# Attention beside eight products instead of eleven: four steps a pair, placed by half products, and two gated products ahead of it and two behind

## The chip, the cores and the metric

The kernel runs on one core of one Trainium2 chip. The metric is the device time of one launch in microseconds (us). A core has TensorE (PE in the profile, with PEld for its weight loads), VectorE (DVE), ScalarE (ACT), GpSimd (POOL) and SyncE (SP, which only issues transfers), and 16 DMA engines that move data between DRAM and the on-chip memory. TensorE writes its sums to eight banks of PSUM.

## What is computed

One layer over 1024 tokens of 1024 channels, all float32. The reference, cut:

```python
h = rmsnorm(x, norm_g)
q, k, v, za, u, vs, zs, gm = split(h @ w_in)
q, k = partial_rope(q), partial_rope(k)           # 16 query heads, 2 key heads, 64 wide
a   = window_sink_attention(q, k, v, sinks)        # 64-token chunks; a chunk sees itself and two before
a   = (a * silu(za)) @ w_att_out
sgo = chunked_spatial_gating(gelu(u), gelu(vs), sg_w, sg_b, ln_g, ln_b)
sgo = (sgo * silu(zs)) @ w_sg_out
ga, gs = split(sigmoid(gm + b_merge))
y = ga * a + gs * sgo
x = x + y @ w_o
return rmsnorm(x, final_g)
```

## The kernel before

**Products.** Every big product is made in pairs of 128 output rows. A pair takes seven half-size products (a seven-product scheme for a 2 by 2 block), named after the right-hand form that each uses: b11, t1, t2, b21, t3, b22, t4. A float32 operand is split into a high and a low part of the reduced type fp32r (lines L155 on ACT and L156 on DVE, results `wh` and `wl`), and `product` (L343, its matmul at L351) adds high x high, high x low and low x high over four blocks of 128: 12 matmuls of 128x512. Two of the weights' parts are used as they are (`r0`, `r1`, loaded to `wr`), two more are sums of parts (`sa`, `sb`, tile `s`), made by DVE (`pair_job`, L251 to L255) or beforehand in DRAM by accumulating transfers on POOL's queue (`early_job`, L300; the steps at L306 are handed out one by one by `part_of_early` and wait for the latest PSUM copy of ACT).

**Order of the stages.** vs; u (gated mixing, gives `s1_dr`); k and v; q; one pair of zs, silu at once and times `s1_dr`; then eleven pairs with attention beside them: the other three pairs of zs (stored raw in `zr_dr`), four of gs, four of ga; then four pairs of za with silu and times the attention (`at_dr`); then the products with w_sg_out, w_att_out and w_o. In the za stage `gate_raw` (L1462) also brings back `zr_dr` and `s1_dr`, takes silu on ACT (L1468), multiplies on POOL (L1472) and stores `s_dr`.

**Attention.** It has 32 steps (2 key heads x 8 blocks of 128 tokens x 2 halves of the heads). A step n is a chain over three engines:

- `scores` (PE L1109, 8 matmuls into two banks `ps_sc`)
- `maxima` (DVE L1134 to L1137, once for each of two chunks c)
- `exponentials` (ACT L1145 to L1153)
- `weigh` (DVE L1158 to L1165: sum, reciprocal and the weights of chunk 0; ACT L1167: chunk 1)
- `turn` (PE L1180, L1185: transposes into the two banks `ps_tp`)
- `casts` (ACT L1196, L1202) and `inner_rest`, `ends_rest` (DVE L1208, L1216): the split into high and low part
- `values` (PE L1233, into one bank `ps_o`)
- `outputs` (ACT copy L1246, DVE add L1247, and every second step a store to `at_dr` on POOL's queue)

`locked_pair` (L1260) writes a pair's seven products and three steps b, c and most of a in a fixed order: PE, ACT and DVE run this part in written order, while the other stages are ordered by a scheduler. Between two products stands whatever PE owes the attention; in front of t2 and b21 for instance:

```python
of(values, a)
mm(acc, 3, "t2", False)
of(weigh, b)
of(outputs, a)
x22 = xtile()
pace[0] = nc.scalar.mul(x22[:], t5, -1.0)
if p:
    split_next()
    ...
of(turn, b)
t2 = bank("o")[:]
mm(t2, 1, "b21", True)
x12 = xtile()
pace[0] = nc.scalar.copy(x12[:], acc)
of(casts, b)
```

The query tile of step n is loaded two steps ahead on SP's queue (two buffers `q`).

Of the kernel before, what the change touches and what calls it, by code (L numbers as in the profile page):

```python
# [31 lines left out]
P = 128  # L32
# [21 lines left out]
def hybrid_tile(  # L54
# [67 lines left out]
    zr_dr = scratch("zr_dr")  # L122
# [71 lines left out]
    sums_to_make = []  # L194
    locked = [False]
# [90 lines left out]

    early = []
# [12 lines left out]
    def early_job(n, i0, i1):  # L300
# [18 lines left out]
        def job():  # L319
            r0, r1 = raw_tile(), raw_tile()  # L320
            sa = mtile([P, D], F32, "s", 2)
            sb = mtile([P, D], F32, "s", 2)
            copy_to(r0[:], w[i0])
            for a, dst in enumerate((sa, sb)):
                copy_to(
                    dst[:].rearrange("p (b n) -> p b n", b=2),
                    made[:].rearrange("p (b a) n -> p a b n", a=2)[:, a],
                )
            copy_to(r1[:, HALF:D], w[i1][:, HALF:D])
            return [  # L330
                (r0[:], [(n, 0), (n, 1)]),
                (sa[:], [(n, 2), (n, 3)]),
                (sb[:], [(n, 4), (n, 5)]),
                (r1[:, HALF:D], [(n, 6)]),
            ]
# [24 lines left out]
    def gemm_pair(b, finish, hook=lambda: None, second="o"):  # L360
# [5 lines left out]
        acc = bank("mm")[:]  # L366
        x11, x12, x22 = xtile(), xtile(), xtile()
        product(acc, ready[n, 0], b["b11"], True)
# [51 lines left out]
    ahead_of = {}  # L420
    for base, step, made in (
        (W_U, 1, 0),
        (W_Q, 0, 0),
        (W_ZS, 1, 0),
        (W_SG, 2, KC),
        (W_ATT, 2, KC),
        (W_ZA, 1, 0),
        (W_SG + 1, 2, KC // 2),
        (W_ATT + 1, 2, KC // 2),
    ):  # L430
        if base == W_Q:
            jobs.append(pair_job(len(jobs), of_kv))
        for m in range(0, KC, 2):
            i0, i1 = base + step * m, base + step * (m + 1)
            if m < made:
                ahead_of[len(jobs)] = True
                jobs.append(early_job(len(jobs), i0, i1))
            else:
                load = of_w(i0, i1) if step else of_token_w(base, m)
                jobs.append(pair_job(len(jobs), load))  # L440
    N_PAIRS = len(jobs)
# [427 lines left out]
    def rope_tables():  # L869

        cos_sb = mtile([P, NT, 16], F32, "cos", 1, pool)
        sin_sb = mtile([P, NT, 16], F32, "sin", 1, pool)
        nc.sync.dma_start(cos_sb[:], cos)
        nc.sync.dma_start(sin_sb[:], sin)
        yield
        for src in (cos_sb[:, :, 0:8], sin_sb[:, :, 8:16]):
            tab = mtile([P, HALF], F32, f"tab{len(tables)}", 1, pool)
            wide = []
            for i in range(4):
                v = mtile([P, 2, 8, 8], F32, "wide", 4, pool)  # L880
                nc.vector.tensor_copy(v[:], src[:, i : i + 5 : 4, :].unsqueeze(2).broadcast_to([P, 2, 8, 8]))
                wide.append(v)
            yield
            pt = bank("tp")
            for i, v in enumerate(wide):
                nc.tensor.transpose(pt[:, i * P : (i + 1) * P], v[:].rearrange("p a h d -> p (a h d)"), ident[:])
# [162 lines left out]
    def first_loads():  # L1049
        for n in range(2):  # L1050
# [4 lines left out]
    gates, silus, hooked = [], [], [0]  # L1055

    def gate_of_zs(i, half, q, src, sign):
        nc.scalar.activation(q[:], src, AF.Silu, scale=sign)
        silus.append((i, half, q))

    def part_of_zs():
        part_of_q()
        hooked[0] += 1
        if hooked[0] == 1:
            two = mtile([P, 2, HALF], F32, "qhl", 3, pool)
            copy_to(two[:].rearrange("p h n -> p (h n)"), s1_dr[0:P, :])
            gates.extend((two[:, 0, :], get(s1_dr, 1, 1, 5, "rot")[:], two[:, 1, :]))
        if hooked[0] == 5:
            gates.append(get(s1_dr, 1, 0, 5, "rot")[:])
        if hooked[0] >= 4:  # L1070
            while silus:
                i, half, q = silus.pop(0)
                nc.vector.tensor_mul(q[:], q[:], gates.pop(0))
                put(s_dr, i, half, q[:])

    steps_of_q += [rotate(1, 1), first_loads()]
    gemm_pair(hb, gate_of_zs, part_of_zs)
# [18 lines left out]
    def scores(n):  # L1096
# [19 lines left out]
        if n + 2 < len(steps):  # L1116
            qT.append(query_stage(*steps[n + 2]))
# [21 lines left out]
    def exponentials(n):  # L1139

        st = held[n]
        for c in range(2):
            lo, hi = window_of(st.t, c)
            for i in range(2):
                nc.scalar.activation(  # L1145
                    st.pr[:, i, place_of(c, lo, hi)],
                    st.sc[c][:, i, lo:hi],
                    AF.Exp,
                    bias=st.nmax[:, c, i : i + 1],
                    scale=-1.0,  # L1150
                    accum_out=st.sums[:, c, i : i + 1],
                )
        nc.scalar.activation(st.es[:], st.es[:], AF.Exp)  # L1153
# [106 lines left out]
    def locked_pair(p, finish):  # L1260


        a, b, c, d = range(3 * p - 1, 3 * p + 3)
# [5 lines left out]
        def mm(acc, at, form, fresh):  # L1269
            product(acc, ready[n, at], hb[form], fresh)  # L1270
            part_of_early(1 if p < 3 else 2)
# [558 lines left out]
```

## Time and profile before

| | |
|---|---|
| median of three runs | 942.9 us (941.05 to 943.75) |
| the profiled execution's own time | 940.39 us |
| its span | 938.4 us, so 2.0 us lie around it |
| PE busy | 909.4 us, 97% |
| DVE / ACT / POOL busy | 691.8 / 529.7 / 150.3 us |
| granted TensorE clock, mean | 0.992 |
| moved by DMA | 212.9 MB |

Busy time of PE is modelled: a matmul of 128x512 is shown about 0.39 us long but the next one starts some 0.23 us later, so a gap on PE shows up about 0.16 us short. In a row of the timeline the first two figures are start and length, and in brackets stands the idle time of the engine just before with what ended it.

### The profile page before, as it was taken

How to read it: one execution, taken by the hardware profiler on the slowest of the kernel's cores; microseconds unless marked ns; L12 is line 12 of the kernel's file. 1: busy time of each engine (PE TensorE's matmuls, PEld its weight loads, DVE VectorE, ACT ScalarE, POOL GpSimd, SP SyncE). 2: the span in 40 equal slices, each digit the busy share in tenths (PEclk: the TensorE clock that was granted, in tenths of full speed). 3: DMA queues.
4: the chain of work that ended last, by engine and by line, in shares of the span. 5: the costliest groups of instructions: out<-in, count | busy, mean ns of one | idle time of the engine just before them, and what ended most of it. 6: DMA issues, size and time to landing. Idle time of an engine off the chain costs nothing.

```text
span 938.4 us, 13120 instructions
## 1 busy us (share of the span) xinstructions
PE 909.4 (97%) x4285; PEld 751.4 (80%) x4285; DVE 691.8 (74%) x1222; ACT 529.7 (56%) x1050; POOL 150.3 (16%) x199
## 2 busy tenths in 40 slices
PE   7999999999999899999999999998999999999996
PEld 5788888888888778888888888876787887878885
DVE  5784776665677677777777777765799689668996
ACT  6873333334445457777667767754385565457443
POOL 1002222213011022211001111024010011210012
PEclk9999999999999999999999999999999999999998
DMA  6237678877688799998888999279888664999623
GB/s 248 100 112 218 197 145 186 184 152 225 232 291 265 220 268 250 254 246 227 260 265 270 226 254 273 73 285 372 305 278 310 213 200 151 261 298 334 203 106 120
DMA packets 130620, 212.91 MB, mean 227 GB/s; under 512 B 12696, under 2 KB 59288, under 8 KB 130552
## 3 DMA queue, kind: packets, MB, share of 16 engines
q1 hardware_dynamic: 110312, 157.28, 50.8%
q0 software_dynamic: 20096, 54.54, 25.3%
q8 instruction: 34, 0.56, 0.3%
q14 instruction: 34, 0.28, 0.1%
q10 hardware_dynamic: 144, 0.26, 0.1%
HBM read 152.13 MB, written 93.45 MB: 262 GB/s over the span
## 4 chain that ended last, share of the span: by engine, by line
PE 46%; DMA 8%; DVE 6%; issue 3%; ACT 2%; SPq 0%; POOL 0%; ACTq 0%; DVEq 0%; POOLq 0%
PE ps_mm L351 20%; PE ps_o L351 15%; PE ps_sc L1109 3%; PE ps_sc L351 2%; PE ps_o L1233 2%; PE ps_tp L351 2%; DMA q<-q_hl 2%; DMA g<-at_dr 1%; PE ps_tp L1180 1%; DVE wl L156 1%; DMA wr<-in_w_dram 1%; DMA s_dr<-bq 1%; DMA bq<-zr_dr 1%; DVE bq L185 1%; DMA v<-v_dr 1%
## 5 line engine op out<-in xcount | busy, mean ns | idle before, releaser
L156 DVE TENSOR_TENSOR wl<-wr,wh 128x1024 fp32r<-128x1024 f32 (+1 forms) x80 | 77.9, 975 | 50.6 <-ACT wh L155 49.8
L155 ACT CAST wh<-s 128x1024 fp32r<-128x1024 f32 (+1 forms) x67 | 66.4, 996 | 83.5 <-PE ps_mm L351 32.4
L155 ACT CAST wh<-wr 128x1024 fp32r<-128x1024 f32 (+1 forms) x80 | 65.5, 829 | 65.6 <-PE ps_mm L351 33.6
L156 DVE TENSOR_TENSOR wl<-s,wh 128x1024 fp32r<-128x1024 f32 (+1 forms) x67 | 77.9, 1164 | 19.2 <-ACT wh L155 19.1
L1145 ACT ACTIVATE pr<-ps_sc,sm 128x192 f32<-128x192 f32 (+2 forms) x128 | 51.3, 408 | 56.2 <-DVE sm L1135 55.4
L351 PE MATMUL ps_mm<-T_b11h,wl 128*128 128x512 f32 x140 | 55.6, 397 | 5.5 <-DVE wl L156 5.5
L306 POOL DMA_DIRECT2D sums<-in_w_dram x48 | 36.3, 957 | 148.4 <-PE ps_mm L587 64.0
L351 PE MATMUL ps_o<-T_t1h,wh 128*128 128x512 f32 x148 | 58.9, 398 | 1.0 <-ACT wh L155 0.9
L351 PE MATMUL ps_o<-T_b22h,wh 128*128 128x512 f32 x148 | 58.4, 395 | 0.0
L351 PE MATMUL ps_o<-T_t1h,wl 128*128 128x512 f32 x148 | 58.1, 393 | 0.2
L351 PE MATMUL ps_o<-T_t1l,wh 128*128 128x512 f32 x148 | 57.9, 391 | 0.0
L351 PE MATMUL ps_o<-T_b22h,wl 128*128 128x512 f32 x148 | 57.8, 391 | 0.0
L351 PE MATMUL ps_o<-T_b22l,wh 128*128 128x512 f32 x148 | 57.8, 391 | 0.0
L351 PE MATMUL ps_mm<-T_b11h,wh 128*128 128x512 f32 x140 | 55.3, 395 | 1.6 <-ACT wh L155 1.6
L351 PE MATMUL ps_mm<-T_t4h,wh 128*128 128x512 f32 x140 | 56.2, 401 | 0.7 <-DVE x L386 0.7
L351 PE MATMUL ps_mm<-T_t4h,wl 128*128 128x512 f32 x140 | 55.3, 395 | 0.0
L351 PE MATMUL ps_mm<-T_t4l,wh 128*128 128x512 f32 x140 | 55.3, 395 | 0.0
L351 PE MATMUL ps_mm<-T_t3h,wh 128*128 128x512 f32 x140 | 55.2, 394 | 0.0
L351 PE MATMUL ps_mm<-T_b11l,wh 128*128 128x512 f32 x140 | 55.1, 394 | 0.0
L351 PE MATMUL ps_mm<-T_t3h,wl 128*128 128x512 f32 x140 | 54.8, 391 | 0.0
L351 PE MATMUL ps_mm<-T_t2h,wl 128*128 128x512 f32 x140 | 54.7, 390 | 0.0
L351 PE MATMUL ps_mm<-T_t2l,wh 128*128 128x512 f32 x140 | 54.6, 390 | 0.0
(365 smaller groups left out, 2474.0 us busy)
## 6 DMA issues: line engine op xcount, KB each, us to landing
wr<-in_w_dram SPq DMA_DIRECT2D x80, 256.0 KB
sums<-in_w_dram POOLq DMA_DIRECT2D x24, 512.0 KB, 5.6
s<-sums SPq DMA_DIRECT2D x24, 512.0 KB
wr<-in_w_dram SPq DMA_DIRECT2D x16, 512.0 KB
q_hl<-qhl SPq DMA_DIRECT2D x16, 512.0 KB
q<-q_hl SPq DMA_DIRECT2D x64, 128.0 KB
y_dr<-x POOLq DMA_DIRECT2D x28, 256.0 KB, 6.1
sums<-in_w_dram POOLq DMA_DIRECT2D x24, 256.0 KB, 9.8
```

What stands on the lines that cost most here:

```text
L155: nc.scalar.copy(hi, src)
L156: return nc.vector.tensor_sub(lo, src, hi.bitcast(F32))
L185: op(dst[:, i : i + 2, :], a[:, i : i + 2, :], c[:, i : i + 2, :])
L306: return lambda: paced(nc.gpsimd.dma_start(dst, src, accum_op=op))
L351: nc.tensor.matmul(acc, lt, rt, start=fresh and k == 0 and n == 0, stop=k == 3 and n == 2, skip_group_check=True,)
L1109: nc.tensor.matmul(sc[:, i, lo:hi], q_of[:, c, i * P : (i + 1) * P], kt[:, f, lo:hi], start=f == 0, stop=f == 1,)
L1145: nc.scalar.activation(st.pr[:, i, place_of(c, lo, hi)], st.sc[c][:, i, lo:hi], AF.Exp, bias=st.nmax[:, c, i : i + 1], scale=-1.0, accum_o ...
L1180: nc.tensor.transpose(st.inner[0:wide, at : at + P], st.pr[:, i, place_of(c, 64 if st.t else P, 192)], ident[:])
L1233: nc.tensor.matmul(st.po[:, cs], lt, rt, start=i == 0, stop=i == len(terms) - 1, skip_group_check=True)
```

## The change

Attention now runs beside the eight pairs of gs and ga alone, four steps a pair. Two pairs of zs stand in front of it and two behind, all with silu at once and the product with `s1_dr` on DVE; `zr_dr`, `gate_raw` and POOL's multiplies are gone. Inside a pair the work of attention is hung at six places: ahead of products and, by the new argument `middle` of `product`, after half of one. `t2` takes an `mm` bank, so that the one free `ps_o` bank serves the attention. The exponentials of a step are issued a chunk at a time. Query tiles are loaded three steps ahead (three buffers). The sums of the third zs pair are made in DRAM as well (13 early jobs instead of 12), seven early steps go beside the second zs pair, and the loads of sums are issued after t2. The tables of the rotation share buffers with `rot`. At the end the first product of the third zs pair stands between the last steps of attention.

The diff, cut to its core:

```diff
-    def product(acc, part, form, fresh, last=True):
+    def product(acc, part, form, fresh, middle=lambda: None):
         for k in range(4):
+            if k == 2:
+                middle()
...
+    add_pairs(W_ZS, 1, (0, 2))
+    add_pairs(W_SG, 2, ALL, True)
+    add_pairs(W_ATT, 2, ALL, True)
+    add_pairs(W_ZS, 1, (4,), True)
+    add_pairs(W_ZS, 1, (6,))
+    add_pairs(W_ZA, 1, ALL)
...
-        qt = mtile([P, 4, P], F32R, "q", 2, aheads)
+        qt = mtile([P, 4, P], F32R, "q", 3, aheads)
...
-    steps_of_q += [rotate(1, 1), first_loads()]
-    gemm_pair(hb, gate_of_zs, part_of_zs)
+    steps_of_q += [first_loads(), rotate(1, 1)]
+    zs_pair(0, part_of_q)
+    zs_pair(2, with_early)
+    after(nc.scalar.activation(warm[:], eps_sb[:], AF.Exp), last_silu[0])
...
-        a, b, c, d = range(3 * p - 1, 3 * p + 3)
+        y, z, a, b, c, d = range(4 * p - 2, 4 * p + 4)
...
-            part_of_early(1 if p < 3 else 2)
+            part_of_early(1 if p < 5 else 2)
...
+        of(scores, a)
+        of(turn, z)
+        of(values, y)
+        def h0():
+            of(outputs, y)
+            of(casts, z)
+            of(inner_rest, z)
+            of(maxima, a, 0)
+            of(ends_rest, z)
+            of(maxima, a, 1)
+            of(exponentials, a, 0)
+            of(exponentials, a, 1)
+        multiply(acc, 0, "b11", True, h0)
+        for tail in tails:
+            tail()
...
+        def h2():
+            of(weigh, a)
+            of(values, z)
+            of(outputs, z)
+            x11 = held["x11"] = xtile()
+            pace[0] = nc.scalar.copy(x11[:], acc)
+            of(scores, b)
+        multiply(t5, 2, "t1", True, h2)
+        of(maxima, b, 0)
+        of(maxima, b, 1)
+        of(exponentials, b, 0)
         of(turn, a)
+        def h4():
+            of(casts, a)
+            of(inner_rest, a)
+            of(exponentials, b, 1)
+            of(ends_rest, a)
+        multiply(acc, 3, "t2", False, h4)
         of(weigh, b)
         if p:
             split_next()
+        load_made()
+        t2 = bank("mm")[:]
+        def h6():
+            x12 = held["x12"] = xtile()
+            pace[0] = nc.scalar.copy(x12[:], acc)
+            of(values, a)
+            of(outputs, a)
+            hold.append(split_next(True))
+            of(turn, b)
+            of(scores, c)
+        multiply(t2, 1, "b21", True, h6)
...
+        multiply(acc, 4, "t3", False, h8)
         of(values, b)
         of(weigh, c)
...
         of(scores, d)
+        def h10():
+            of(maxima, d, 0)
+            of(maxima, d, 1)
+            of(exponentials, d, 0)
+            of(turn, c)
+            hold.pop()()
+        multiply(t5, 5, "b22", False, h10)
+        of(exponentials, d, 1)
+        of(casts, c)
+        of(weigh, d)
...
-        for dst in (zr_dr, gs_dr, ga_dr):
-            for m in range(2 if dst is zr_dr else 0, KC, 2):
+        for dst in (gs_dr, ga_dr):
+            for m in range(0, KC, 2):
                 locked_pair(p, rest(dst, m))
...
-            nc.gpsimd.tensor_tensor(z[:, 0:2, :], z[:, 0:2, :], z[:, 2:4, :], op=ALU.mult)
-            copy_to(s_dr[j * P : (j + 1) * P, :], z[:, 0:2, :].rearrange("p h n -> p (h n)"))
...
+    want_gates(s1_dr, 4)
+    silu_pair(4, s_dr, (s1_dr, 6))
+    silu_pair(6, s_dr, (at_dr, 0))
     for m in range(0, KC, 2):
...
+        silu_pair(m, a_dr, (at_dr, m + 2) if m < 6 else None)
```

What this does to the order of the engines is shown at three places. The first is ACT, early in a pair of the middle of attention. Before, from the tail of the pair in front (`x` from `ps_mm`, L490) over the copy of an output (L1246), a copy of a sum (L1295), the casts of one step and the exponentials of the next to that step's weighing (L1167):

```order
L490 ACTIVATE x_4954<-ps_mm_4627 128x512
L1246 COPY aT_4836<-ps_o_4929 64x2x4x64
L1295 COPY x_5004<-ps_mm_4934 128x512
L1196 CAST pT_5006<-ps_tp_4965 128x512
L1202 CAST pTb_5008<-ps_tp_4970 64x256 x2
L1145 ACTIVATE pr_4990,sm_4987<-ps_sc_4973,sm_4986 128x192 x2
L1145 ACTIVATE pr_4990,sm_4987<-ps_sc_4978,sm_4986 128x192 x2
L1153 ACTIVATE sm_4988<-sm_4988 128x4
L1167 ACTIVATE pr_4990<-pr_4990,sm_4989 128x192 x2
```

And now the same stretch for steps z, a and b of the second pair (L1275 is the copy of an output, L1334 of a sum, L1173 exponentials, L1225 and L1231 casts, L1196 the weighing, L154 the cast of a split):

```order
L1275 COPY aT_3293<-ps_o_3348 64x2x4x64
L1334 COPY x_3361<-ps_mm_3266 128x512
L1173 ACTIVATE pr_3382,sm_3379<-ps_sc_3363,sm_3378 128x192 x2
L1225 CAST pT_3411<-ps_tp_3397 128x512
L1231 CAST pTb_3413<-ps_tp_3402 64x256 x2
L1173 ACTIVATE pr_3382,sm_3379<-ps_sc_3368,sm_3378 128x192 x2
L1182 ACTIVATE sm_3380<-sm_3380 128x4
L1196 ACTIVATE pr_3382<-pr_3382,sm_3381 128x192 x2
L154 CAST wh_3435<-s_2915 128x1024
```

The first chunk's exponentials have moved ahead of the casts of the step before. The second place is PE around the product b21 of the same kind of pair. Before, the transposes of step b (L1180, L1185) stand alone ahead of the product:

```order
L351 MATMUL ps_mm_4627<-T_t2l_781,wh_4603 128x512
L351 MATMUL ps_mm_4627<-T_t2h_780,wl_4604 128x512
L1180 MATMUL ps_tp_4754<-ident,pr_4678 128x128 x4
L1185 MATMUL ps_tp_4759<-ident,pr_4678 128x128 x2
L351 MATMUL ps_o_4762<-T_b21h_143,wh_4520 128x512
```

Now, in the middle of the product, stand the values of a (L1262), the transposes of b (L1209, L1214) and the scores of c (L1138):

```order
L364 MATMUL ps_mm_3443<-T_b21h_143,wl_3175 128x512
L1262 MATMUL ps_o_3453<-pT_3411,vi_3171 128x512 x2
L1262 MATMUL ps_o_3453<-pTb_3413,v_3168 128x256 x2
L1209 MATMUL ps_tp_3463<-ident,pr_3382 128x128 x4
L1214 MATMUL ps_tp_3468<-ident,pr_3382 128x128 x2
L1138 MATMUL ps_sc_3471<-k_3187,q_3189 128x192 x4
L1138 MATMUL ps_sc_3476<-k_3187,q_3189 128x192 x4
L364 MATMUL ps_mm_3443<-T_b21h_143,wh_3174 128x512
```

Three groups that stood apart are now one, half a product later. The third place is ACT in the first pair after attention. Before, silu of the raw zs (`bq`, L1468) stands among silu of za (`x`, L1490) and the casts of splits (`wh`):

```order
L376 COPY x_6187<-ps_mm_6185 128x512
L1468 ACT_TABLE_LOAD
L1468 ACTIVATE bq_6176<-bq_6176 128x1024
L1490 ACTIVATE x_6186<-x_6186 128x512
L155 CAST wh_6268<-wr_6157 128x1024
L1468 ACTIVATE bq_6179<-bq_6179 128x1024
L1490 ACTIVATE x_6188<-x_6188 128x512
L155 CAST wh_6314<-s_6239 128x1024
```

Now the same place holds the third pair of zs, with silu on its own sums (L1527):

```order
L392 COPY x_5945<-ps_mm_5886 128x512
L154 CAST wh_6004<-wr_5519 128x1024
L1527 ACT_TABLE_LOAD
L1527 ACTIVATE x_5944<-x_5944 128x512
L1527 ACTIVATE x_5946<-x_5946 128x512
L154 CAST wh_6050<-s_5979 128x1024
L1527 ACTIVATE x_5945<-x_5945 128x512
L154 CAST wh_6072<-s_5982 128x1024
```

The silu of raw zs has gone from this place, and with it the loads that it read.

More of the change, by code (lines that the diff above doesn't have):

```diff
@@ L1283, in locked_pair @@
         tails.clear()
-        of(outputs, a - 1)
-        if p:
-            make_sums(None, 1)
-        if by_dve and p:
-            begin_job()
-        of(turn, a)
-        of(scores, b)
-        t5 = bank("o")[:]
-        mm(t5, 2, "t1", True)
-        x11 = xtile()
-        pace[0] = nc.scalar.copy(x11[:], acc)
-        of(casts, a)
-        of(inner_rest, a)
-        of(maxima, b, 0)
-        of(ends_rest, a)
-        of(maxima, b, 1)
-        of(exponentials, b)
-        of(values, a)
```

270 lines of the change are left out of this document (128 added, 142 removed).

## The prediction

> **What bounds the kernel now.** I read the page first, then busy time by stage, then the timeline of PE where a stage is not full, and last ACT and DVE inside one pair of attention.
>
> ```profile
> PE 909.4 (97%) x4285; PEld 751.4 (80%) x4285; DVE 691.8 (74%) x1222; ACT 529.7 (56%) x1050; POOL 150.3 (16%) x199
> 320.00:330.00 10.00, 7.99 (x31) 6.52 (x32) 8.53 (x15) 4.07 (x7) 0.81 (x1) 0.83 0.70 218
> 416.00:590.00 174.00, 174.00 (x916) 148.05 (x916) 131.03 (x306) 124.42 (x352) 23.27 (x31) 1.00 0.88 245
> 630.00:640.00 10.00, 6.99 (x24) 4.85 (x23) 10.00 (x6) 5.08 (x7) 7.38 (x3) 0.83 1.01 375
> 650.00:660.00 10.00, 7.85 (x34) 5.88 (x33) 5.75 (x9) 3.00 (x5) 2.41 (x1) 1.00 1.00 384
> ```
>
> PE is the bound: 909 of 938 us. The stage rows give length, then PE, PEld, DVE, ACT and POOL busy, the granted clock, the share of the DMA engines and GB/s. In 174 us in the middle of attention PE is never idle, while DVE is busy 131 us and ACT 124 us. No matmul of any size is added or taken away by the change, so all it can win is PE's idle and slow time, and all it can lose is new idle time. Two places that it touches are not full. The entry into attention:
>
> ```profile
> 321.75 0.31 PE L1109 MATMUL ps_sc<-k,q 128*128 128x64 f32 x1 [2.76 <-DMA q<-q_hl]
> 322.31 0.66 PE L351 MATMUL ps_mm<-T_t4h,wh 128*128 128x512 f32 x1 [0.26 <-DVE x L386]
> 326.76 0.93 PE L1109 MATMUL ps_sc<-k,q 128*128 128x64 f32 x7
> 334.17 0.65 PE L1180 MATMUL ps_tp<-ident,pr 128*64 128x128 f32 x4 [0.96 <-PE ps_mm L351]
> 354.21 1.16 PE L1109 MATMUL ps_sc<-k,q 128*128 128x192 f32 x8 [0.86 <-DMA q<-q_hl]
> 381.52 1.17 PE L1109 MATMUL ps_sc<-k,q 128*128 128x192 f32 x8 [0.95 <-DMA v<-v_dr]
> ```
>
> The first scores waited 2.76 us for their query tile, and the 12 matmuls of t4 behind them took from 322.31 to 326.76, 4.45 us, at a low clock. And the stage behind attention:
>
> ```profile
> 635.21 0.50 PE L351 MATMUL ps_mm<-T_b11h,wl 128*128 128x512 f32 x1 [2.91 <-DVE wl L156]
> 657.64 0.50 PE L351 MATMUL ps_mm<-T_b11h,wh 128*128 128x512 f32 x1 [1.62 <-ACT wh L155]
> 658.90 0.50 PE L351 MATMUL ps_mm<-T_b11h,wl 128*128 128x512 f32 x1 [0.53 <-DVE wl L156]
> 661.84 0.50 PE L351 MATMUL ps_o<-T_t1h,wh 128*128 128x512 f32 x1 [0.37 <-ACT wh L155]
> 629.37 2.48 DVE L1491 TENSOR_TENSOR x<-x,g 128x512 f32<-128x512 f32 x1 [2.24 <-ACT x L1490]
> 631.78 3.38 DVE L156 TENSOR_TENSOR wl<-wr,wh 128x1024 fp32r<-128x1024 f32 x1
> 638.46 1.21 DVE L156 TENSOR_TENSOR wl<-s,wh 128x1024 fp32r<-128x1024 f32 x1
> 628.90 8.49 POOL L1472 TENSOR_TENSOR bq<-bq 128x1024 f32<-128x1024 f32 x3 [13.73 <-DMA bq<-s_dr]
> ```
>
> PE waits 2.91 us for a split on DVE. That split took 3.38 us, nearly three times the 1.21 us of one of the same size at 638.46, and beside it POOL multiplies raw zs, 8.49 us from 628.90 on; the product with the gate, 2.48 us, is stretched too (0.69 us for one of 128x512, row 614.16 below). The later waits of 1.62, 0.53 and 0.37 us follow in the next pair, with raw zs, its gates and the weights sharing DMA engines that are full (shares of 1.01 and 1.00).
>
> **What is won.** At the entry the brackets sum to 2.76 + 0.26 + 0.96 + 0.86 + 0.95 = 5.8 us, and some 0.16 us is hidden under each (a matmul is shown 0.39 us long, the next starts 0.23 later), 0.8 in five. The low clock cost 4.45 less the 2.75 us of a product at full clock (row 563.54 below): 1.7. Together 8.3 us. Behind attention: 2.91 + 1.62 + 0.53 + 0.37 = 5.4, four times 0.16 = 0.6, and a clock of 0.83 over 10 us another 1.7: 7.8 us. In all 16.1.
>
> At the entry the first three query tiles are now loaded ahead of the second rotation and two pairs of zs lie behind them, so the first wait and its low clock go. From the first scores to their transposes PE had 5.5 us (t1 and t2); it now has b11, t1 and the next scores, 6.4 us, so the wait of 0.96 goes. Behind attention POOL has no multiply left, the first two pairs are gated by `s1_dr`, which has lain in DRAM since the mixing, and za's gates are asked for a pair ahead. What I leave standing are the waits for later loads at 354 and 381 us (0.86 + 0.95 + 0.3 = 2.1): a third buffer helps, but four steps now fall to a pair where three did. So 14.0 us are won. Between nothing and 16.1 as bounds, I take a value near the upper end, since the row behind each larger gap names a cause that the change removes.
>
> **What is paid inside attention.** A pair now holds four steps.
>
> ```profile
> 560.79 0.39 PE L351 MATMUL ps_mm<-T_b11h,wh 128*128 128x512 f32 x1
> 563.54 0.60 PE L1180 MATMUL ps_tp<-ident,pr 128*128 128x128 f32 x4
> 564.11 1.17 PE L1109 MATMUL ps_sc<-k,q 128*128 128x192 f32 x8
> 565.12 0.41 PE L351 MATMUL ps_o<-T_t1h,wh 128*128 128x512 f32 x1
> 567.87 0.62 PE L1233 MATMUL ps_o<-pT,vi 128*128 128x512 f32 x2
> 568.57 0.39 PE L351 MATMUL ps_mm<-T_t2h,wh 128*128 128x512 f32 x1
> 587.03 0.39 PE L351 MATMUL ps_mm<-T_b11h,wh 128*128 128x512 f32 x1
> ```
>
> By starts: a product 2.75 us, transposes 0.57, scores 1.01, values 0.70, so 2.28 a step; a pair 26.24, of which 7 x 2.75 + 3 x 2.28 = 26.1 are explained and 0.15 is switching. Four steps make 28.4 + 0.15 = 28.5. The 32 steps cost PE the same as before: halving a product costs nothing as long as nobody is late.
>
> Somebody is, I think. In a pair ACT and DVE have these links, by rows of before (values to copy to add to the next DVE operation first, then one step from its rest to its weighing):
>
> ```profile
> 611.82 0.39 PE L1233 MATMUL ps_o<-pT,vi 128*128 128x512 f32 x1
> 612.81 0.58 ACT L1246 COPY aT<-ps_o 64x512 f32<-64x512 f32 x1 [0.42 <-PE ps_o L1233]
> 613.44 0.69 DVE L1247 TENSOR_TENSOR aT<-aT,ps_o 64x512 f32<-64x512 f32 x1
> 614.16 0.69 DVE L251 TENSOR_TENSOR s<-wr,wr 128x512 f32<-128x512 f32 x1
> 512.16 0.59 ACT L1196 CAST pT<-ps_tp 128x512 fp32r<-128x512 f32 x1
> 512.64 0.75 ACT L1202 CAST pTb<-ps_tp 64x256 fp32r<-64x256 f32 x2
> 512.79 0.69 DVE L1208 TENSOR_TENSOR pT<-ps_tp,pT 128x512 fp32r<-128x512 f32 x1 [0.41 <-ACT pT L1196]
> 513.40 0.55 DVE L1134 TENSOR_REDUCE sm<-ps_sc 128x2 f32<-128x384 f32 x1
> 514.24 0.42 ACT L1145 ACTIVATE pr<-ps_sc,sm 128x192 f32<-128x192 f32 x1 [0.84 <-DVE sm L1135]
> 515.91 0.42 ACT L1145 ACTIVATE pr<-ps_sc,sm 128x192 f32<-128x192 f32 x1 [0.76 <-DVE sm L1135]
> 516.72 0.20 ACT L1153 ACTIVATE sm<-sm 128x4 f32<-128x4 f32 x1
> 516.95 0.17 DVE L1158 TENSOR_TENSOR sm<-sm,sm 128x4 f32<-128x4 f32 x1 [0.94 <-ACT sm L1153]
> 517.42 0.80 ACT L1167 ACTIVATE pr<-pr,sm 128x192 f32<-128x192 f32 x2 [0.50 <-DVE sm L1159]
> 518.25 0.58 ACT L1246 COPY aT<-ps_o 64x512 f32<-64x512 f32 x1
> ```
>
> I walk a pair from its start. Scores of a end at 1.0, transposes of z at 1.6, values of y run from 1.6; b11, half of t1, values of z, scores of b, the other half: PE wants to transpose a at 9.5. The new order on DVE is: add of y, rest of z, maxima of a around the ends of z, as it stood before. Values to copy 0.99, to add 0.63, to the rest 0.72, from there (512.79) to the end of a's weighing (518.22) 5.43: 1.6 + 7.8 = 9.4. In time, by a hair. Next PE does the transposes, t2, half of b21 and values of a, and wants to transpose b at 14.9. But from 9.4 the chain runs: copy of z 0.05 later, add 0.63, maximum of b 0.72, exponentials 0.84 (513.40 to 514.24) and 0.81 long, the casts of a that now stand between b's two chunks 1.23 (512.16 to 513.39), second exponentials 0.81, the sinks' 0.23, sum and reciprocal to the weighing 0.47, weighing 0.80: 6.6, so 16.0. PE waits 1.05 us there, in the middle of b21, and the scores of c, t3 and all behind wait with it. Carrying the walk on with the same rows, the rest of b is 0.3 late for the values of b; everything else is in time, and DVE and ACT end the pair just early enough for the next. So 1.35 us a pair, 29.9 instead of 28.5. The first pair has no y and z; of seven others one has two steps with short windows: 9.0 us. The bounds are 0 (no link is late) and rival C. At the end, two steps are left over against one, and the values of the last must wait for casts behind one product: 0.5 us by the same links (0.99 + 0.6 + 0.6 + 1.2 + 0.45 against 0.7 + 2.75).
>
> Of the rest: the thirteenth early job and zs weights are DMA work in a share of 0.88, the two zs pairs in front have DVE and ACT as lightly used as the query pairs, and the products of silu and gate move from POOL to DVE (twelve of 0.7 us; DVE is busy 8.5 of 10 us in the row from 320 and 5.8 in that from 650). I put these at 0, hidden by PE's products; if DVE has no room there, they cost up to 8 us.
>
> Sum against the profiled execution: 940.4 - 14.0 + 9.0 + 0.5 = 935.9, 4.5 us less. The median lies at 942.9; the same difference gives **938.4**.
>
> **The rivals.**
> A, the forecast: 42%.
> B, attention keeps up: the links overlap better than my walk, as in the 174 us without a wait. Then 942.9 - 14.0 + 0.5 = 929.4. 17%.
> C, slower: ACT and DVE already hand work to and fro nearly without pause. DVE's 131 of 174 us are 19.8 a pair of 26.24, 75%. A step costs DVE 3.2 (512.79 to 516.01) + 1.0 for weighing + 0.6 for the add, so a pair of four 24.6; if 75% is all that such a chain lets DVE do, a pair lasts 32.6, 4.1 over, seven times 28: 942.9 - 13.5 + 28 = 957. It decides from 1.9 us a pair (13.5 / 7), a pair of 30.4. Against it: my walk has DVE at 82%, since the exponentials are cut in two. 24%.
> D, the gaps at both ends do not close, but move: attention is denser in transfers and early steps run at full pace through five pairs instead of three. With half of 14 kept, 945.4. 13%.
> E, the clock: small gaps on PE lower it. After the gap of 1.62 us the row 650 to 660 shows 1.00; only behind gaps of 2.76 and 2.91 stands 0.83. If each pair paid 1.7 us, seven would be 12: 950. 4%. The Trainium skill, "TensorE: Matmul & The Clock Gate", section "A second HAM failure mode: psum-queue depth-cycling", says that a PE which idles briefly between groups of matmuls, cycling through PSUM banks, can swing between half and full clock; by that this rival would be the likely one, and the trace so far does not agree.
>
> **How the numbers follow.** A difference under 0.3%, 2.8 us, is about what a measurement of this kernel cannot tell from none. Faster: 33 of A's 42, and B: 50%. Same: 9 of A, 7 of D, 4 of C: 20%. Slower: 20 of C, 6 of D, 4 of E: 30%. The range from 929 to 953 leaves out part of B and the upper half of C. A alone would be 934 to 942.
>
> **What would show it.** In the new profile: no wait for q above 1 us at the entry and clock 1.00 there; DVE's product with the gate at 0.7 us behind attention; pairs of attention 29.9 us apart, with a wait of about 1 us at the transposes inside b21, released by the weighing (L1196). Pairs of 28.5 are B, of 30.4 and more C; low clock in attention is E; waits for DMA at scores or splits are D. I am wrong if the change in span does not come from these three places.

## The result, and the profile after

The changed kernel takes 943.56 us (median of 20 runs, 941.24 to 947.03), the kernel before 942.17 us beside it (20 runs, 939.30 to 946.65): a ratio of 1.0016, 95% interval 1.0004 to 1.0028. Under 0.3%, so no difference that counts. The profiled execution took 942.91 us with a span of 941.1, against 940.39 and 938.4.

The page's first row shows as much work on PE as before:

```profile
PE 911.0 (97%) x4285; PEld 753.0 (80%) x4285; DVE 690.3 (73%) x1230; ACT 530.5 (56%) x1054; POOL 147.2 (16%) x215
```

By stage (length, then PE, PEld, DVE, ACT and POOL busy, granted clock, share of the DMA engines, GB/s) the stretch behind attention has closed, and a new hole stands at the entry:

```profile
340.00:350.00 10.00, 3.53 (x16) 2.57 (x14) 0.27 (x1) 1.36 (x2) 0.00 (x0) 0.85 0.92 303
350.00:360.00 10.00, 5.08 (x18) 4.24 (x19) 6.40 (x19) 3.26 (x16) 1.24 (x2) 0.50 0.86 271
...
630.00:640.00 10.00, 10.00 (x46) 8.29 (x45) 6.03 (x9) 3.54 (x6) 0.48 (x1) 1.00 0.87 296
```

In the hole every engine is nearly idle. The timeline of each, read from PE back to who released it:

```profile
354.92 1.97 PE L1138 MATMUL ps_sc<-k,q 128*128 128x64 f32 x8 [11.39 <-ACT pr L1173]
354.16 0.31 ACT L1173 ACTIVATE pr<-ps_sc,sm 128x64 f32<-128x64 f32 x1 [12.79 <-DVE sm L1164]
349.73 0.69 DVE L1094 TENSOR_TENSOR x<-x,qhl 128x512 f32<-128x512 f32 x1 [11.83 <-DMA qhl<-s_dr]
332.17 0.53 SPq L201 DMA_DIRECT2D qhl<-s_dr  x1
```

The scores of attention's second step wait for the banks of the first step's scores, whose exponentials wait for DVE's maxima; those stand behind the product of silu and gate (L1094) of the second zs pair, and that product waits 11.83 us for its gate, asked for at 332.17 and there at 349.7, 17.5 us later. Behind the hole the clock is 0.50, and eight scores take 1.97 us.

Inside attention PE's rows show pairs 29.53 us apart (410.10 to 439.63):

```profile
410.10 0.40 PE L364 MATMUL ps_mm<-T_b11h,wh 128*128 128x512 f32 x1
423.12 0.74 PE L1209 MATMUL ps_tp<-ident,pr 128*128 128x128 f32 x4
437.86 0.60 PE L1209 MATMUL ps_tp<-ident,pr 128*128 128x128 f32 x4
438.68 0.41 PE L1214 MATMUL ps_tp<-ident,pr 128*128 128x128 f32 x2 [0.21 <-DVE pTb L1245]
439.63 0.40 PE L364 MATMUL ps_mm<-T_b11h,wh 128*128 128x512 f32 x1
...
583.96 0.66 PE L1209 MATMUL ps_tp<-ident,pr 128*128 128x128 f32 x4 [0.61 <-DVE pT L1237]
```

The transposes of b inside b21 (423.12) wait for nobody. The one wait that recurs lies at the pair's end, between the two parts of the transposes of z (437.86 to 438.68: 0.82 us, where 0.38 is their pace), until DVE has read the ends of c. Once, at attention's end, PE waits 0.61 us (583.96).

An account of all PE rows: the time from each row's start to the next, less what its matmuls take at full clock (0.227 us for 128x512, 0.0945 a transpose, 0.126 a score, 0.12 the rest), summed by stretch. "Lost" means this sum from here on.

| PE time lost, us | before | after |
| --- | --- | --- |
| from 300 to 360 (entry into attention) | 8.2 | 14.4 |
| rest of attention, its tail included (to 612; to 590) | 4.5 | 10.8 |
| behind it (to 690) | 8.9 | -0.1 |
| rest of the program | 16.6 | 15.9 |

The sum rises by 2.8 us, the span by 2.7. About 9 us were won behind attention, and 6 each paid at the entry and inside.

### The profile page after: what moved, and what is told of

Its sections match the earlier page's. It is cut to its first block, busy times and chain, and to the rows that moved or that the text cites. A ratio compares the mean times of both kernels' runs of the same rounds, so it can differ in the third digit from the quotient of the medians.

```text
span 941.1 us, 13141 instructions
## 1 busy us (share of the span) xinstructions
PE 911.0 (97%) x4285; PEld 753.0 (80%) x4285; DVE 690.3 (73%) x1230; ACT 530.5 (56%) x1054; POOL 147.2 (16%) x215
## 4 chain that ended last, share of the span: by engine, by line
PE 36%; DVE 14%; ACT 7%; issue 4%; DMA 1%; ACTq 0%; DVEq 0%
PE ps_mm L364 17%; PE ps_o L364 11%; PE ps_tp L364 3%; ACT pr L1173 2%; PE ps_sc L364 2%; DVE sm L1163 2%; DVE aT L1276 1%; DVE pTb L1245 1%; ACT pr L1196 1%; DVE wl L155 1%; PE ps_sc L1138 1%; DVE bq L184 1%; PE ps_o L1262 1%; ACT aT L1275 1%; DVE pT L1237 1%
## 5 line engine op out<-in xcount | busy, mean ns | idle before, releaser
L154 ACT CAST wh<-s 128x1024 fp32r<-128x1024 f32 (+1 forms) x78 | 77.9, 1002 | 82.7 <-PE ps_mm L364 39.9
L155 DVE TENSOR_TENSOR wl<-s,wh 128x1024 fp32r<-128x1024 f32 (+1 forms) x78 | 91.4, 1172 | 21.8 <-ACT wh L154 21.7
L155 DVE TENSOR_TENSOR wl<-wr,wh 128x1024 fp32r<-128x1024 f32 (+1 forms) x64 | 60.3, 945 | 61.3 <-ACT wh L154 61.3
L154 ACT CAST wh<-wr 128x1024 fp32r<-128x1024 f32 (+1 forms) x64 | 53.0, 830 | 78.0 <-PE ps_mm L364 37.5
L1173 ACT ACTIVATE pr<-ps_sc,sm 128x192 f32<-128x192 f32 (+2 forms) x128 | 51.3, 408 | 42.9 <-DVE sm L1164 34.8
L310 POOL DMA_DIRECT2D sums<-in_w_dram x52 | 39.5, 968 | 191.9 <-PE ps_mm L604 64.0
L364 PE MATMUL ps_mm<-T_t2h,wh 128*128 128x512 f32 x140 | 55.6, 397 | 0.1
```

Source lines behind the costliest of these rows:

```text
L154: nc.scalar.copy(hi, src)
L155: return nc.vector.tensor_sub(lo, src, hi.bitcast(F32))
L310: return lambda: paced(nc.gpsimd.dma_start(dst, src, accum_op=op))
L364: nc.tensor.matmul(acc, lt, rt, start=fresh and k == 0 and n == 0, stop=k == 3 and n == 2, skip_group_check=True,)
L1173: nc.scalar.activation(st.pr[:, i, place_of(c, lo, hi)], st.sc[c][:, i, lo:hi], AF.Exp, bias=st.nmax[:, c, i : i + 1], scale=-1.0, accum_o ...
```

## The experiments

Theory D says that the DMA engines are full at the entry: whatever transfer comes last there is late, and the queue of an engine that computes in order makes that a stop for PE. Theory G says that it is this one gate. Two more questions were what a pair of attention is bound by, and whether POOL's multiply was the cause of the gaps behind attention. Ratios are to the kernel before on the same chip.

| run | ratio, 95% interval | lost 340 to 360 | what else |
| --- | --- | --- | --- |
| changed kernel | 1.0016 (1.0004 to 1.0028) | 14.1 | |
| second pair's gates not loaded | 0.9944 (0.9924 to 0.9964) | 10.5 | |
| POOL's steps taken out there | 0.9877 (0.9842 to 0.9912) | 3.7 | 3.7 at 540 |
| gates asked for earlier, ACT's queue | 0.9944 (0.9922 to 0.9967) | 11.6 | |
| products behind attention on POOL | 0.9987 (0.9971 to 1.0004) | 14.7 | none behind |
| split behind the maxima of d | 1.0011 (0.9997 to 1.0026) | 15.5 | 4.4 at 430 to 450 |
| steps out, the last eight behind attention | 1.0003 (0.9989 to 1.0017) | 4.7 | 12.2 at 590 to 630 |
| the three together | 0.9975 (0.9964 to 0.9986) | 0.2 | 12.2 at 590 to 620 |
| wide multiplies on POOL added | one run, 947.47 us | 14.3 | 2.6 at 600 |
| split behind the ends of b | 1.0043 (1.0020 to 1.0066) | 14.3 | 6.5 at 430 to 450 |
| gates and steps, eight beside za | **0.9859** (0.9839 to 0.9879) | 0.1 | 3.7 at 700 |
| gates and steps, 22 beside za and gs, one sum unfinished | 0.9964 (0.9941 to 0.9989) | 0.2 | 12.7 at 720 to 740 |
| gates and steps, eight beside gs | 0.9935 (0.9912 to 0.9959) | 0.3 | 9.2 at 720 to 740 |

Beside the four runs after the first the kernel before had a median of 945.6 us, beside the others 942.2 to 943.1, so ratios of different sets compare to about 0.3%; the losses in the traces do not hang on this.

**The second pair's gates are not loaded.**

```
-            if hooked[0] == 1:              # loads of gates, in both pairs
+            if m and hooked[0] == 1:
+                gates.extend([tables[0][:]] * 4)
+            if m == 0 and hooked[0] == 1:
```

> Leaves out the loads of the four gates of the second pair of zs in front of attention; its products multiply by a tile that is resident, so part of the output is not the reference's. Theory G (late gate): in the changed kernel the first product with a gate of that pair is at the head of DVE's queue at 337.9 and waits 11.83 us for its gate, which was asked for at 332.17; the maxima of step 0 stand behind it on DVE, ACT's exponentials wait for them 12.79 us and PE's second scores 11.39 us for a bank. Without the loads the wait of 11.39 goes, and the slow clock behind it (2.7 us in the rows from 350): about 14 us less than the changed kernel, 929.5. Rival X (the exponentials are late by themselves: table load of 1.28 us at 339.88, two banks for scores): the gap stays at 8 us or more, and the time within 3 us of the changed kernel, 940 to 944. Rival D (full DMA engines): the 1 MB that is not loaded helps something, but the wait goes over to the next load (the splits' weights, the queries): a gap of 4 us or more there, 934 to 939.

PE's and DVE's rows of this kernel at the hole:

```profile
350.29 1.97 PE L1140 MATMUL ps_sc<-k,q 128*128 128x64 f32 x8 [7.15 <-ACT pr L1175]
348.89 0.29 DVE L1165 TENSOR_REDUCE sm<-ps_sc 128x2 f32<-128x128 f32 x1 [8.05 <-DMA s_dr<-x]
330.55 0.57 SPq L919 DMA_DIRECT2D q_hl<-qhl  x1
348.64 0.64 SPq L1058 DMA_DIRECT2D q<-q_hl  x1
```

With no gate to wait for, the hole is still 7.15 us. The maxima now wait by themselves for SP's queue, and for stores, not for a load. In the kernel their tiles (`sm`) lie in attention's memory pool, which is opened where the pool of the queries has just been closed, so the first maxima have to wait until the rotated queries have been stored from there. The last of four such stores (L919) is asked for at 330.55; SP's next transfer on the same semaphore, the load at 348.64, waits until it has landed, so it was 18 us under way, and the maxima start 0.25 us after that. (The store `s_dr<-x` that the row names is a guess by the profile; the link over the pool is read from the kernel and the semaphores, not tested by a run.) G alone is out: the gate was only the last of a row of late transfers. Rival X is out too: ACT's table load ends at 340.79, over 8 us before the exponentials, which wait for these maxima. D had 934 to 939, and 0.9944 of about 942 is 937.

**POOL's seven steps of the sums leave the second zs pair.**

```
     def with_early():
         part_of_q()
-        part_of_early(1)
-            part_of_early(1 if p < 5 else 2)
+            part_of_early(1 if p < 7 else 2)
```

> The changed kernel, but the seven steps of the sums that POOL issues beside the second zs pair are taken out of it and issued inside attention (a step a product through seven pairs instead of five). Theory G1 (the load of the gate is late because the DMA engines are full: share 1.06 and 0.92 in the rows from 330, a third of the packets' time POOL's): the load lands some 6 us earlier, the gap on PE of 11.4 falls to 3 to 6, and the time by 6 to 10 us, 934 to 938. Theory G2 (it is late by its place in SP's queue, behind two stores of the rotation, two loads of sums and a store): it is still asked for at about 332 and the gap stays at 9 us or more, the time within 3 us of the changed kernel. Against both: with the steps moved into attention, splits there may wait for their sums, +1 to +5.

```profile
344.98 1.39 PE L1137 MATMUL ps_sc<-k,q 128*128 128x64 f32 x8 [1.39 <-ACT pr L1172]
339.79 0.69 DVE L1094 TENSOR_TENSOR x<-x,qhl 128x512 f32<-128x512 f32 x1 [1.82 <-DMA qhl<-s_dr]
331.78 0.43 SPq L201 DMA_DIRECT2D qhl<-s_dr  x1
544.72 1.90 PE L1137 MATMUL ps_sc<-k,q 128*128 128x192 f32 x8 [1.87 <-ACT wh L154]
```

The gate is asked for as before (331.78) and lands after 8.0 us instead of 17.5; the hole shrinks from 11.39 to 1.39 us. The view of the DMA queues says why. From 330 to 345, for the changed kernel and then for this one (packets, MB, share of 16 engines; q1 is SP's queue, q0 POOL's):

```profile
q0 software_dynamic: 852, 2.36, 66.3%
q1 hardware_dynamic: 955, 1.92, 39.5%
```

```profile
q1 hardware_dynamic: 2039, 4.28, 79.5%
q0 software_dynamic: 144, 0.26, 11.5%
```

In these 15 us SP's queue moved 1.92 MB there and 4.28 MB here. POOL's sums took two thirds of the engines' time while everything that attention's start needs stood in SP's queue. This is G1, stronger than it was expected, and G2 is out: the place in the queue is the same. The Trainium skill, "DMA: Bandwidth & Descriptors", section "SWDGE vs HWDGE vs iDMA", states that each DMA engine takes turns between the queues that feed it. That both queues moved side by side agrees; how the turns are shared out no run here shows (852 to 955 packets, but 66.3% to 39.5% of the time).

Full engines alone make no hole, though. The kernel before had them too (stages as above, the last figures but one are the DMA shares):

```profile
330.00:340.00 10.00, 9.04 (x48) 7.31 (x47) 4.78 (x15) 6.74 (x18) 4.16 (x6) 1.00 1.01 240
340.00:350.00 10.00, 9.59 (x51) 7.84 (x50) 9.00 (x22) 5.49 (x19) 0.00 (x0) 1.00 1.02 267
350.00:360.00 10.00, 9.14 (x48) 7.61 (x47) 6.72 (x19) 7.14 (x24) 1.34 (x2) 1.00 1.06 343
```

It moved 6.8 MB from 330 to 355, the changed kernel 7.1, and it lost only 3 us from 330 to 360. What is new is that transfers which cannot wait now fall into such a stretch: the gates of the last zs pair are asked for at 332 (before at 310), the last rotated queries stored from 328 on (before from 319), and attention's maxima stand behind both on DVE.

**The gates are asked for earlier, two of them on ACT's queue.**

```
+            if m == 0 and hooked[0] in (1, 5):      # both wide tiles in the first pair
...
+            if m and hooked[0] in (2, 3):
+                nc.scalar.dma_start(g[:], place(s1_dr, m + 1, 3 - hooked[0]))
```

> The changed kernel with the same loads in another place: the gates' wide tile of the second zs pair is asked for in the fifth hook of the first pair (SP, at about 316), ahead of the rotation's stores, and the two narrow tiles on ACT's own queue after t1 and t2 (about 326 and 329). Theory G2 (place in SP's queue): the gates are there by 337, the gap of 11.39 and the slow clock behind it go, about 12 to 14 us less, 929 to 932. Theory G1 (the engines are full whatever the order): the same bytes have to pass in the same stretch, so that either the gates still land late or the sums and the weights do; a gap of 5 us or more stays between 335 and 360, and the time falls by less than 7.

```profile
341.36 1.05 ACT L154 CAST wh<-s 128x1024 fp32r<-128x1024 f32 x1 [7.00 <-DMA s<-sums]
347.38 1.04 ACT L154 CAST wh<-s 128x1024 fp32r<-128x1024 f32 x1 [4.45 <-DMA s<-sums]
352.80 1.97 PE L1146 MATMUL ps_sc<-k,q 128*128 128x64 f32 x8 [7.89 <-ACT pr L1181]
```

The products no longer wait for a gate, but ACT waits 7.00 and 4.45 us for the sums of the next weights, which used to be there in time, and PE 7.89 us. The wait went from one transfer to another, as G1 had it. By the ratios, place in a queue alone gives about half of what the steps gave, though the loss from 340 to 360 falls only from 14.1 to 11.6.

**Behind attention the products of silu and gate go to POOL.**

```
-            nc.vector.tensor_mul(q[:], q[:], gates.pop(0)[:])
+            (nc.gpsimd if dst is s_dr else nc.vector).tensor_mul(q[:], q[:], gates.pop(0)[:])
```

> The changed kernel, but behind attention the products of silu and gate of the two zs pairs are made by POOL and not by DVE. Theory P (as predicted: a multiply on POOL stretches DVE's operations beside it, 1.21 to 3.38 us for a split, 0.69 to 2.48 for a product, and PE waited for that): DVE's splits there go from 1.22 to 2 us and more, PE, which has no gap from 590 to 690, gets waits for wl of 1 us and more, and the time rises by 2 to 8 us. Rival L (the gaps there came from loads of raw zs and gates at a DMA share of 1.0): PE stays busy 10.00 of 10 us, and the time is within 1.5 us of the changed kernel.

The stage, and one split on DVE with the multiply on POOL that overlaps it:

```profile
620.00:630.00 10.00, 10.00 (x46) 8.29 (x45) 3.35 (x4) 4.35 (x6) 7.15 (x7) 1.00 0.70 225
623.10 1.23 DVE L155 TENSOR_TENSOR wl<-s,wh 128x1024 fp32r<-128x1024 f32 x1 [0.17 <-ACT wh L154]
623.68 1.79 POOL L1528 TENSOR_TENSOR x<-x,g 128x512 f32<-128x512 f32 x1 [0.58 <-ACT x L1527]
```

PE stays full. DVE's split keeps its 1.23 us, and here it is POOL's multiply that is longer (1.79 against 1.28 for one with nothing beside it). The expectation of theory P was wrong for this form, and rival L's came true. So the form of the kernel before was tried.

**Three multiplies of 128x1024 on POOL, read by nobody.**

```
+    wide = mtile([P, 4, HALF], F32, "bq", 4, pool)[:, 0:2, :]
...
+            nc.gpsimd.tensor_mul(wide, wide, wide)      # three times
```

> The changed kernel with three multiplies of 128x1024 in place on POOL, on a tile nobody reads, added behind attention from 591 on (the form of the raw multiply of the kernel before, 8.49 us for three). Theory P: DVE's operations beside them are stretched as at 629 to 637 of the kernel before: 0.69 to about 2.5, 1.22 to about 3.4, and back at their length when POOL is done. Rival L (those rows were stretched by something else, such as transfers at a share of 1.0): they stay within 0.1 us of their length beside POOL's multiplies.

```profile
598.49 6.86 POOL L1527 TENSOR_TENSOR bq<-bq 128x1024 f32<-128x1024 f32 x3
598.92 2.38 DVE L251 TENSOR_TENSOR s<-wr,wr 128x512 f32<-128x512 f32 x1
601.22 2.38 DVE L255 TENSOR_TENSOR s<-s,wr 128x512 f32<-128x512 f32 x1
603.63 0.69 DVE L397 TENSOR_TENSOR x<-x,ps_tp 128x512 f32<-128x512 f32 x1
607.69 0.51 PE L364 MATMUL ps_mm<-T_t4h,wh 128*128 128x512 f32 x1 [2.29 <-DVE x L402]
```

Theory P holds for this form: DVE's operations of 0.69 us take 2.38 each, about one multiply of POOL (6.86 / 3 = 2.29), and PE waits 2.29 us. The operation that reads PSUM (ps_tp, 603.63) keeps its 0.69 us beside POOL's third. DVE does not share with POOL here, it waits for the end of what runs. The Trainium skill, "SBUF — State Buffer", section "SBUF: two separate sides", calls it an exclusive lock which the first holds for its whole instruction; these rows agree.

**The split that DVE owes stands behind the maxima of d; then, behind the ends of b.**

```
         of(outputs, b)
-        hold.pop()()
...
             of(maxima, d, 1)
+            hold.pop(0)()           # first run;  second run: behind of(ends_rest, b)
```

> The changed kernel with one thing moved in each pair of attention: the split that DVE owed from before the scores of d (wl, at 432.66) stands behind the maxima of d and not ahead of them. In the changed kernel a pair lasts 29.52 us, 1.15 more than its matmuls at full pace, and 0.44 of that lies at one place, between the two parts of the transposes at the pair's start, where PE waits for the rest of c's ends on DVE (L1245). Theory A (that chain is what is late: maxima of d at 433.38, exponentials at 434.23, then casts, weighing and the rests, one behind the other): all of it starts about 0.7 us earlier, the 0.44 goes from seven pairs, a pair lasts 29.1 and the time falls by 3 us. Rival B (the chain is bound elsewhere, or the split is now what a product waits for): pairs stay at 29.5, or a wait for wl of 0.3 us and more stands at b22 or t4; time within 1 us of the changed kernel or above it.

> The changed kernel with the owed split on DVE moved the other way: it stands behind the rest of the ends of b (428.54 to 429.40 in the changed kernel's pair), ahead of the add of x11, and no longer between the output of b and the maxima of d. Theory A (DVE's chain of maxima, exponentials, casts and rests of c and d is late by this one split): that chain starts 0.7 us earlier and no product waits for the split, so neither the 0.44 between the two parts of the transposes nor a wait in t4 is left; a pair lasts 29.1 and the time falls by 3 us. Rival B (four steps cost what they cost in changes between products and attention on PE): 29.4 to 29.5 a pair and the time within 1 us. The entry is as in the changed kernel (gap of 11 to 13 us).

PE's rows of a pair in the first run, and of the fourth pair's first scores in the second:

```profile
530.62 0.40 PE L364 MATMUL ps_mm<-T_b11h,wh 128*128 128x512 f32 x1
555.43 0.51 PE L364 MATMUL ps_mm<-T_t4h,wl 128*128 128x512 f32 x1
560.15 0.40 PE L364 MATMUL ps_mm<-T_b11h,wh 128*128 128x512 f32 x1
```

```profile
441.51 1.99 PE L1138 MATMUL ps_sc<-k,q 128*128 128x192 f32 x8 [3.58 <-DMA q<-q_hl]
```

Theory A falls in both by the length of the pairs. In the first run the 0.44 at the transposes is gone and t4 is 0.4 longer, since its low weights (555.43) now come late; the pair stays at 29.53. In the second it stays where it was, at 29.51 a pair, because the weighing of c and the output of b behind it start later by the same 0.7. Wherever those 0.7 us of DVE stand, something that PE needs comes 0.4 late: this part of the pair is bound by the chain between DVE and ACT. The other 0.7 of the 1.15 over the matmuls' own 28.4 is spread over the changes between products and attention. That the second run is slower, I cannot put down to the split: its profile shows a query 3.58 us late at 441.51, which hangs on transfers. The first run's profile has the same wait at the same place, 1.78 us, and its one pair there lasts 33.13; so the times of these two runs say little on the split, and why the queries are late in both stays open.

**Steps taken out, the rest behind attention; and the three changes together.**

```
-            part_of_early(1 if p < 5 else 2)
+            part_of_early(1 if p < 4 else 2)
...
+        if early:                   # in the silu pairs behind attention
+            early.pop(0)()
```

> As with the seven steps taken out from beside the second zs pair, but the last ten steps of the sums (those for the output's weights, which are read far later) are issued behind attention, so that attention keeps its pace of a step a product through four pairs and half of that after. Theory D (the DMA engines are full at the entry; whatever is taken out of that stretch shortens the gap): the gap stays at 1 to 2 us as in that run, and the 2.02 us at 544, where the steps had been pushed into pairs six and seven, goes: 1 to 3 us less than that run, ratio to before 0.985. Rival: the 2 us at 544 were from the queries and keys on SP, and they stay; or the steps behind attention (share 0.71 to 1.02 there) make splits late: ratio 0.988 or above.

> The changed kernel with three things together: the steps of the sums taken out from beside the second zs pair and the last ten issued behind attention; that pair's gates asked for earlier and on ACT's queue; the owed split behind the maxima of d. Theory D and A: no gap over 1 us between 300 and 360, pairs of 29.1, and 16 to 18 us less than the changed kernel: ratio to before 0.981 to 0.983. Rival: with POOL's traffic gone the gates' place is worth nothing more, and the pairs stay at 29.5: ratio 0.986 and above.

The rest is eight steps by POOL's rows (L480, the last of them at 618), not ten as the expectations here and below say, nor seven as the last one says. DVE and PE behind attention in the first of these runs, and the stages of the second:

```profile
614.01 0.69 DVE L254 TENSOR_TENSOR s<-wr 128x512 f32<-128x512 f32 x1 [12.01 <-DMA wr<-in_w_dram]
616.62 0.80 PE L364 MATMUL ps_mm<-T_t3h,wl 128*128 128x512 f32 x1 [7.58 <-DVE wl L155]
```

```profile
340.00:350.00 10.00, 10.00 (x57) 8.54 (x55) 4.57 (x20) 6.58 (x27) 2.92 (x4) 1.00 1.05 282
...
600.00:610.00 10.00, 3.49 (x16) 2.56 (x14) 2.20 (x3) 2.15 (x3) 0.00 (x0) 0.89 1.02 356
```

With gates and steps both moved, the entry loses 0.2 us: it is closed, at a full clock and a DMA share of 1.05. But the eight steps put behind attention made raw weights 12 us late there. A step of the sums costs where a load with a near deadline shares the engines with it.

**Gates and steps, with the steps in three other places.** Eight beside the za pairs from the second on (with the split behind the ends of b), all 16 steps of the output's sums beside za and gs (16, not the 24 of its expectation), and eight beside gs, with the split where it was. The second of these also issues the last six steps of other sums there (L310, 635 to 658). One of them belongs to the third zs pair, which is over by then, so that its product is made with unfinished sums.

> The changed kernel with the second zs pair's gates asked for earlier and on ACT's queue, no step of the sums beside that pair, the last ten steps issued from the second za pair on, one in two products (share of the DMA engines 0.47 to 0.64 there), and the owed split behind the ends of b. Theory D: no gap at the entry as in the run of three changes, and none behind attention, where the ten steps had cost about 10 us; with the pairs at 29.1 the time is 17 to 19 us under the changed kernel, ratio to before 0.980 to 0.984. Rival: the steps on POOL's queue hold up the stores that stand behind them, and so the x tiles, and PE waits in the za or gs pairs; ratio 0.985 or above.

> As the run before it, but all 24 steps of the sums for the output's weights leave attention and are issued from the second za pair on, one in two products, through the gs pairs. Theory: attention, with a share of 0.9 to 1.1 of the DMA engines, has room, so that loads of queries, keys and sums are never late: 1 to 2 us less than the run with ten. Rival: 24 steps of 12 to 15 us each on POOL's queue are too many for the stores behind them, and the time rises by 2 us or more against the run with ten.

> The changed kernel with two things alone: the second zs pair's gates asked for earlier and on ACT's queue, and no step of the sums beside that pair; the last seven steps (seven, not ten as counted in the expectations before) are issued beside the gs pairs, one in three products (share of the DMA engines about 0.6 there). The owed split stands as in the changed kernel. Theory D: the gap at the entry is gone (under 0.5 us), pairs last 29.5 as in every variant so far, and without the 2 us that the seven steps cost at 704 in the run with them beside the za pairs the time is 928 to 930, ratio to before 0.983 to 0.986. Rival: the seven steps hold up the stores of y on POOL's queue and PE waits in the gs pairs, as with 16 of them: 931 or more. If the owed split had its part in that run's time, 0.5 to 1 us is missing here.

The stages at the entry and behind attention in the first, PE in the second, DVE and PE in the third:

```profile
340.00:350.00 10.00, 10.00 (x53) 8.41 (x52) 6.10 (x22) 7.67 (x29) 1.68 (x2) 1.00 1.03 321
600.00:610.00 10.00, 10.00 (x46) 8.29 (x45) 7.70 (x10) 4.51 (x7) 1.08 (x2) 1.00 0.56 185
```

```profile
732.91 0.80 PE L364 MATMUL ps_mm<-T_t4h,wh 128*128 128x512 f32 x1 [9.61 <-DVE x L402]
```

```profile
724.75 0.69 DVE L254 TENSOR_TENSOR s<-wr 128x512 f32<-128x512 f32 x1 [8.27 <-DMA wr<-in_w_dram]
730.24 0.79 PE L364 MATMUL ps_mm<-T_t4h,wh 128*128 128x512 f32 x1 [7.21 <-DVE x L402]
```

The first closes both places and is the fastest version (the split that was moved in it had won nothing alone; its steps cost some 2 us at 700 to 710, where the DMA share is 1.00), 930.25 us against 943.07 of the kernel before beside it, and by the ratios about 1.6% under the changed kernel. Beside gs the steps cost 9 us: a raw weight comes 8.27 us late. The expected hold-up of POOL's own stores is not what the rows show; it is D once more. The mean share of about 0.6 on which I chose that stage said little, because it has a stretch at 1.01 of its own (720 to 730 of the changed kernel), just where the weights are fetched.

## Why the prediction was wrong

Forecast were 4.5 us less than before; measured were 1.4 more on the medians (2.5 on the profiled executions). By its steps:

- **The entry, won 8.3 less the 2.1 left standing: wrong, by some 12 us.** The waits for queries did go, those at 354 and 381 included. The step that failed is the sentence that put the early job's and the zs weights' DMA work "at 0", hidden by PE's products, on a share of 0.88. That share is of another stretch (416 to 590); at the entry the kernel before already had 1.01 to 1.06. The loads of the second pair's gates, and what stands behind them on DVE, were not counted at all. The first of them landed 17.5 us after it was asked for, and PE lost 14.4 us at the entry where it had lost 8.2 and 2 were forecast.
- **Behind attention, won 7.8: right, 8.9.** The product with the gate takes 0.69 us on DVE as predicted, and PE is full from 590 to 690. That a wide multiply on POOL stretches DVE by the factor seen before, and makes PE wait, is shown by adding one; how much of the 8.9 was POOL and how much the raw loads in a full share was not separated.
- **Paid in attention 9.0: too much by 2 to 4, place wrong.** A full pair takes 29.53, predicted 29.9; over the 28.5 of the prediction that is 1.0 each, 7 in seven pairs, and by the account above some 5 (10.8 less 4.5, less the tail). The 1.05 at the transposes of b inside b21 is not there: that chain was in time. What is late is c's rest at the pair's end, by 0.4. That the size came within a factor of two, from another place, is luck.
- **Tail 0.5: about 1.2.** PE's rows from 580 to 590 lose 1.8 us, before 0.6 at the corresponding place (600 to 620).
- **The rivals.** D is what happened, at the place of the entry: the gap moved, onto a DMA. Its 945.4 for the median is 1.8 from the 943.56 measured, and it had 13%. The number is near by luck: D kept half of what was to be won at both ends, but the end behind attention closed wholly and the entry lost more than before. C's mechanism, DVE and ACT in turn, binds the pair by 0.4 us, not 4.1. E: in attention from 370 on, with waits of 0.2 to 0.6 us, the granted clock stays at 1.00. Low clock stood behind single gaps: 0.50 behind that of 11.39, 0.84 behind that of 1.39 in the run without POOL's steps (340 to 350), though the 1.62 of before had left it at 1.00.

What the prediction named to look for was sound, except that it looked for waits for q and for DMA at splits. The wait was for DMA at the product with a gate, two engines away from PE.

## What to carry to other kernels

A load moved ahead of a stage needs its bytes counted against what else is on the DMA engines in that very stretch, not against a mean over another one: here, at shares of 0.9 to 1.06, background transfers on another queue doubled the time of a load with a deadline (17.5 us against 8.0). Where an engine works in written order, an operation waiting for such a load stops all that stands behind it, so ask of each load not only whether it is early in its queue, but what stands behind its first reader. A store counts as well, where its memory is to be used again. When one late transfer is cured and the time hardly moves, look for the next one late in the same stretch before looking elsewhere.

## What was not expected of the hardware

- Beside accumulating transfers on POOL's queue, which took 66.3% of the DMA engines' time from 330 to 345, 512 KB asked for on SP's queue took 17.5 us to land; with POOL's queue at 11.5% it took 8.0.
- A long operation on POOL with operands in SBUF (2.29 us) makes one of DVE's with both operands there wait for its end (0.69 becomes 2.38), while an operation of DVE with an operand in PSUM passes (0.69).
